# Routing's selections in float16, their keys spread by GpSimd, row constants from the host, the gates' steps placed later

## The chip, the cores and the metric

The kernel runs on one core of a Trainium2 chip. The metric is the device time of one execution in microseconds (us), the median of three runs. The engines are TensorE (PE, matrix products), VectorE (DVE), ScalarE (ACT), GpSimd (POOL) and SyncE (SP, which here only issues transfers). Each runs its own instructions in the order in which they were built, and waits for the others by semaphores.

## The reference, cut to what matters

A Conformer-like block, a block with a product-key mixture of experts (PEER), and two further layers run over 256 tokens of width 1024. The change touches the PEER part alone:

```python
sc = einsum("bshcd,hcnd->bshcn", q, sub_keys)     # 8 heads, 2 halves, 128 keys
s_top, i_top = top_k(sc, 16)
cand = s_top[..., 0, :, None] + s_top[..., 1, None, :]
cand_idx = i_top[..., 0, :, None] * 128 + i_top[..., 1, None, :]
best, pos = top_k(cand.reshape(..., 256), 16)
expert_idx = take_along_axis(cand_idx.reshape(..., 256), pos)
gate = softmax(best)                              # 8 x 16 experts for each token
a = gelu(einsum("ced,cd->ce", u_emb[expert_idx], h))
out = einsum("ce,ced->cd", gate * a, v_emb[expert_idx])
```

## The kernel before

**Stages of the PEER part.** First the *query stage*: 16 chunks of `w_peer_q`, 24 matmuls each. Each weight tile is split into a rounded part `whi` (ACT) and a rest `wlo` (POOL, L145, three buffers); the third matmul of a chunk reads `wlo`. From the chunks PE forms scores `sc` (L922). Then the *U stage*: 128 blocks of 128 experts, 8 matmuls each with tokens 0 to 159 (`ublock`, L1020), each with one 512 KB transfer into a ring of ten buffers. Then the *V stage*: 128 blocks of `vv` in the same way (`vmm`, L1130), added into four PSUM tiles that are first set to zero by a matmul (L1135).

**Tokens 160 to 255** don't go through the blocks. Two `RowGroup`s (64 and 32 tokens) fetch their experts' rows by indirect DMA on POOL (L1627, 512 KB each, 96 of `un` and 96 of `vv`, eight buffers). DVE forms a dot product for each row of `un` (`junk`, L1632) and adds each row of `vv` to `acc` (L1642). `some_rows` steps them along: RU rows for a U block, RV for a V block.

**The routing** is DVE's. For each head and half of the tokens (`tt`) a `unit` finds two top-16 lists (`max`, `max_index`, `match_replace`; values `tv`, indices `iu`), copies the indices as float32 into `tops` (L862), adds the lists to candidates `cd` (L869) and finds their top 16 (`best`, `pos`). For four heads at a time `select` turns `pos` into two digits `f` and looks up the keys: an equality with 0 to 15 (`eq`, L900), a product with `tops` (L904) and a sum over 16 (L906) into `isel` and `jsel`. For `tt` = 0 the product is POOL's. `gates(tt)` forms the expert number `ei` and the gate `ex`.

**What sets the order.** `self.bg` is a list of generators. After each block, `pump` draws from the first of them until the credits of their `yield`s use up a budget: QP for a query chunk, UP[0] for a U block until the rows are asked for, UP[1] after that. `later(n, fn)` puts a step behind the n-th block from then on. By GL these are `ask` and `exp` (GL[0]), `softmax` (GL[1]) and `turn` (GL[2]). `ask` multiplies `ei` by `spread` on PE (L1617), and DVE makes of it the row numbers `idf`, `idx`. `turn` multiplies `ex` by `spread` (L1617) and transposes `jsel`, `isel` and `ex` (L975). From the first U block to the last V block but five, `in_order` pins every engine to the order in which the code was written.

**Behind the routing** DVE and ACT build one-hot factors (`QO`, P, R) for tokens 0 to 159, PE multiplies them (`place`, L1058, 40 groups), and the gates are multiplied into G (L1068, L1035).

Of the kernel before, what the change touches and what calls it, by code (L numbers as in the profile page):

```python
# [15 lines left out]
ALU = mybir.AluOpType  # L16
AX = mybir.AxisListType
# [22 lines left out]
CST = {}  # L40
# [33 lines left out]
QP = 2.8  # L74
UP = (2.1, 1.4)

RU = 0.8
RV = 0.8

GL = (2, 3, 4)  # L80

NT = 4
G_SCALE = 2.0 ** 15


ROWS = ((192, 64), (160, 32))
N = ROWS[-1][0]

# [3 lines left out]
class Kernel:  # L92
# [725 lines left out]
    def peer(self):  # L818
        nc, a = self.nc, self.a
        p2h, p2t, p2q = self.p2h, self.p2t, self.p2q  # L820
# [29 lines left out]
        pos = p2t.tile([128, 2, 8, 16], U32, name="pos")  # L850
        tops = p2t.tile([128, 2, 2, 8, 16], F32, name="tops")

        def unit(tt, h, scs):
# [20 lines left out]

        def select(tt, h0, eng):

            nh = 4
            ps = pos[:, tt, h0:h0 + nh].rearrange("p h s -> p (h s)")
            m = nh * 16
            q = p2t.tile([128, 4, m], U32, name="q", bufs=1)  # L880
            f = p2t.tile([128, 4, m], F32, name="f", bufs=1)
            nc.vector.tensor_scalar(q[:, 0], ps, 4, None, op0=ALU.logical_shift_right)
# [3 lines left out]
            nc.vector.tensor_copy(f, q)  # L886
            z = p2t.tile([128, m], F32, name="z", bufs=1)
            nc.vector.tensor_scalar(z, f[:, 0], 4.0, None, op0=ALU.is_ge)
# [7 lines left out]
            nc.vector.tensor_add(f[:, 1], f[:, 2], f[:, 3])  # L896
            yield 1.2
            for c, dst in ((0, isel), (1, jsel)):
                eq = p2t.tile([128, m, 16], F32, name="eq", bufs=1)
                nc.vector.tensor_tensor(eq, f[:, c, :, None].to_broadcast([128, m, 16]),  # L900
                                  self.iota[:, None, :16].to_broadcast([128, m, 16]), op=ALU.is_equal)
                yield 1.1
                e4 = eq.rearrange("p (h s) a -> p h s a", s=16)
                eng.tensor_tensor(e4, e4, tops[:, tt, c, h0:h0 + nh, None, :].to_broadcast([128, nh, 16, 16]), op=ALU.mult)  # L904
                yield 1.1
                nc.vector.reduce_sum(dst[:, tt, h0:h0 + nh].rearrange("p h s -> p (h s)"), eq, axis=AX.X)  # L906
                yield 1.1

# [179 lines left out]
        pgb = self.open("pgb", side="right")  # L1088
# [488 lines left out]
class RowGroup:  # L1577
# [3 lines left out]
    def __init__(self, k, pool, hn, ei, ex, t0, n):  # L1581
# [9 lines left out]
        self.w = pool.tile([128, n], F32, name=f"w{t0}")  # L1591
        self.fold = pool.tile([128, n], F32, name=f"fold{t0}")
        nc.vector.reduce_sum(self.fold, k.ident.rearrange("p (c t) -> p t c", t=n), axis=AX.X)
        self.own = pool.tile([128, self.copies], F32, name=f"own{t0}")
        nc.vector.reduce_sum(self.own, k.ident.rearrange("p (c t) -> p c t", t=n), axis=AX.X)
# [110 lines left out]
def _constants():  # L1706
# [3 lines left out]
    def put(name, v):  # L1710
        c[:v.shape[0], CST[name]:CST[name] + v.shape[1]] = v
# [134 lines left out]
```

## Time and profile before

| | us |
|---|---|
| median of three runs (lowest to highest) | 1649.78 (1649.56 to 1651.78) |
| the profiled execution's own time | 1649.49 |
| its span | 1647.4 |
| PE busy | 1563.3 |
| DVE busy | 1176.5 |
| ACT, POOL busy | 649.1, 509.9 |

The page gives each engine's busy time, the granted clock of PE and what the transfers moved in slices of the span; queries of the trace give single instructions, waits with their releasers, and stretches. On the span's time scale the query stage ends at about 342 us, the U stage runs from 344 to 674 us and the V stage from 678 to about 980 us. A raw U or V block is recorded twice for each matmul, so "x32" of L1020 is two blocks. Times of a row of a timeline are the start and the duration.

### The profile page before, as it was taken

How to read it: one execution, taken by the hardware profiler on the slowest of the kernel's cores; microseconds unless marked ns; L12 is line 12 of the kernel's file. 1: busy time of each engine (PE TensorE's matmuls, PEld its weight loads, DVE VectorE, ACT ScalarE, POOL GpSimd, SP SyncE). 2: the span in 40 equal slices, each digit the busy share in tenths (PEclk: the TensorE clock that was granted, in tenths of full speed). 3: DMA queues.
4: the chain of work that ended last, by engine and by line, in shares of the span. 5: the costliest groups of instructions: out<-in, count | busy, mean ns of one | idle time of the engine just before them, and what ended most of it. 6: DMA issues, size and time to landing. Idle time of an engine off the chain costs nothing.

```text
span 1647.4 us, 29860 instructions
## 1 busy us (share of the span) xinstructions
PE 1563.3 (95%) x11502; PEld 1485.5 (90%) x11502; DVE 1176.5 (71%) x2549; ACT 649.1 (39%) x1387; POOL 509.9 (31%) x379
## 2 busy tenths in 40 slices
PE   8989979996899999899979999999999999999998
PEld 7878879996899999899979999888999998899986
DVE  6989988999888889644434448866767557676655
ACT  4557645431155444000000015555554455555543
POOL 3734631611576677545354511000000030000000
PEclk9989989998999999999989999999999999999999
DMA  5522336465999999999999965733655576255553
GB/s 184 168 89 91 129 117 214 169 231 222 355 348 400 400 394 388 359 409 409 408 363 408 409 271 182 245 101 98 224 182 186 184 194 210 91 192 182 183 187 114
DMA packets 109389, 398.97 MB, mean 242 GB/s; under 512 B 12484, under 2 KB 12643, under 8 KB 108736
## 3 DMA queue, kind: packets, MB, share of 16 engines
q1 hardware_dynamic: 73872, 266.37, 46.1%
q0 software_dynamic: 35232, 130.64, 21.1%
q8 instruction: 90, 1.47, 0.4%
q14 instruction: 51, 0.42, 0.1%
q10 hardware_dynamic: 144, 0.07, 0.0%
HBM read 394.86 MB, written 6.11 MB: 243 GB/s over the span
## 4 chain that ended last, share of the span: by engine, by line
PE 71%; DVE 17%; DMA 7%; issue 3%; POOL 2%; ACT 1%; SPq 0%; POOLq 0%; DVEq 0%; ACTq 0%
PE ax L1130 12%; PE mm L1020 12%; PE mm L166 11%; PE mm L167 11%; PE mm L168 11%; DMA raw<-vv 3%; DMA wlo<-vv 3%; DVE ax L610 2%; PE mm L234 2%; PE mm L232 1%; PE mm L233 1%; PE ax L463 1%; DVE wlo L147 1%; PE ax L1058 1%; PE ax L1376 1%
## 5 line engine op out<-in xcount | busy, mean ns | idle before, releaser
L143 ACT ACTIVATE whi<-raw 128x1024 fp32r<-128x1024 f32 x275 | 290.2, 1058 | 616.3 <-DMA raw<-wst 302.5
L147 DVE TENSOR_TENSOR wlo<-raw,whi 128x1024 fp32r<-128x1024 f32 x211 | 257.8, 1224 | 106.8 <-ACT whi L143 103.1
L166 PE MATMUL mm<-xgh,whi 128*128 128x256 f32 x1064 | 305.2, 287 | 0.0
L167 PE MATMUL mm<-xgl,whi 128*128 128x256 f32 x1064 | 302.2, 284 | 2.6 <-DVE xgl L406 2.6
L168 PE MATMUL mm<-xgh,wlo 128*128 128x256 f32 x1064 | 302.4, 284 | 0.3 <-DVE wlo L147 0.3
L1642 DVE SCALAR_TENSOR_TENSOR acc<-row,w,acc 128x1024 f32<-128x1024 f32 x94 | 120.8, 1285 | 156.0 <-DMA row<-vv,idx 155.7
L167 PEld LDWEIGHTS mm<-xgl,whi 128*128 128x128 f32 x1064 | 202.8, 191 | 2.9 <-DVE xgl L406 2.8
L166 PEld LDWEIGHTS mm<-xgh,whi 128*128 128x128 f32 x1064 | 202.7, 191 | 1.1 <-issue 0.8
L168 PEld LDWEIGHTS mm<-xgh,wlo 128*128 128x128 f32 x1064 | 202.5, 190 | 0.6 <-DVE wlo L147 0.5
L145 POOL TENSOR_TENSOR wlo<-raw,whi 128x1024 fp32r<-128x1024 f32 x64 | 153.6, 2405 | 137.7 <-ACT whi L143 134.9
L1627 POOL DMA_INDIRECT row<-vv,idx x96 | 120.6, 1256 | 80.0 <-DMA row<-vv,idx 51.8
L1627 POOL DMA_INDIRECT row<-un,idx x96 | 110.0, 1146 | 108.2 <-DVE idf L1621 54.3
L1130 PE MATMUL ax<-G,raw 128*128 128x160 f32 x832 | 125.5, 306 | 6.8 <-DMA raw<-vv 6.8
L1130 PEld LDWEIGHTS ax<-G,raw 128*128 128x128 f32 x832 | 118.6, 195 | 7.6 <-DMA raw<-vv 7.5
L1632 DVE CUSTOM_DVE_ANT_0 junk<-row,h 128x1024 f32<-128x1024 f32 x96 | 120.4, 1254 | 0.5
L1020 PE MATMUL mm<-hn,raw 128*128 128x160 f32 x816 | 118.8, 300 | 0.0
L1020 PEld LDWEIGHTS mm<-hn,raw 128*128 128x128 f32 x816 | 112.8, 190 | 0.0
L167 PE MATMUL mm<-hl,whi 128*128 128x256 f32 x368 | 107.0, 291 | 2.2 <-DVE hl L377 2.1
L1130 PE MATMUL ax<-G,wlo 128*128 128x160 f32 x608 | 93.5, 307 | 11.0 <-DMA wlo<-vv 11.0
L1130 PEld LDWEIGHTS ax<-G,wlo 128*128 128x128 f32 x608 | 88.1, 196 | 12.1 <-DMA wlo<-vv 11.9
L610 DVE SCALAR_TENSOR_TENSOR ax<-u,cw,ax 128x256 f32<-128x256 f32 x227 | 97.7, 481 | 0.7
L166 PE MATMUL mm<-hh,whi 128*128 128x256 f32 x304 | 90.3, 297 | 2.7 <-DVE u L630 2.2
(439 smaller groups left out, 3436.3 us busy)
## 6 DMA issues: line engine op xcount, KB each, us to landing
raw<-wst SPq DMA_DIRECT2D x278, 512.0 KB, 3.6
raw<-ut SPq DMA_DIRECT2D x51, 512.0 KB, 7.3
raw<-vv SPq DMA_DIRECT2D x40, 512.0 KB, 7.3
whi<-ut SPq DMA_DIRECT2D x39, 512.0 KB, 7.0
wlo<-ut SPq DMA_DIRECT2D x38, 512.0 KB, 7.4
whi<-vv SPq DMA_DIRECT2D x32, 512.0 KB, 7.5
wlo<-vv SPq DMA_DIRECT2D x25, 512.0 KB, 7.6
wlo<-vv POOLq DMA_DIRECT2D x13, 512.0 KB, 16.5
```

The source lines that it names most:

```text
L143: nc.scalar.activation(hi, raw, AF.Copy)
L145: nc.gpsimd.tensor_sub(lo, raw, hi)
L147: self.pin = nc.vector.tensor_sub(lo, raw, hi)
L166: nc.tensor.matmul(pt, w[:, s], xs[0][:, k], start=first, stop=False)
L167: nc.tensor.matmul(pt, w[:, s], xs[1][:, k], start=False, stop=False)
L168: nc.tensor.matmul(pt, lo[:, s], xs[0][:, k], start=False, stop=last)
L610: nc.vector.scalar_tensor_tensor(y[:, c] if k == 30 else ps, u[:, c, k:k + T], cw[:, c, k:k + 1], ps, op0=ALU.mult, op1=ALU.add)
L1020: nc.tensor.matmul(pt, raw[:, k * 128:(k + 1) * 128], hn[:, k, :N], start=(k == 0), stop=(k == C - 1))
L1130: nc.tensor.matmul(acc[d // 2][:, d % 2, :N], raw[:, d * 128:(d + 1) * 128], G(i), start=False, stop=False, skip_group_check=True)
L1627: self.k.nc.gpsimd.indirect_dma_start(t, None, table, bass.IndirectOffsetOnAxis(ap=self.idx[:, s:s + 1], axis=0))
L1632: self.k.nc.vector.tensor_tensor_reduce(junk, row, self.h, 1.0, 0.0, ALU.mult, ALU.add, self.a[:, s:s + 1])
L1642: self.k.nc.vector.scalar_tensor_tensor(self.acc, row, w, self.acc, op0=ALU.mult, op1=ALU.add)
```

## The change

The selections are in float16: `f`, `z`, `eq`, and `tops`, which now has each index sixteen times over, so that all operands of the equality and the product lie side by side in memory. POOL writes `tops` (one cast of 128 x 256 for each top-16 list) and a table `num` in place of `iota`. The sum over 16 is four additions. Both halves of the tokens take all of it on DVE. `spread`, `fold` and `own` come from the host in two transfers issued by ACT. `zero` is set by POOL ahead of the stage, and the four matmuls of 512 columns that clear PSUM are sixteen of 128. GL is (5, 6, 7) for (2, 3, 4), UP[1] 1.1 for 1.4, RU 0.85 for 0.8, RV 0.78 for 0.8.

```diff
-UP = (2.1, 1.4)
-RU = 0.8
-RV = 0.8
-GL = (2, 3, 4)
+UP = (2.1, 1.1)
+RU = 0.85
+RV = 0.78
+GL = (5, 6, 7)
...
+        zero = self.cp.tile([128, 128], F32R, name="zero")
+        nc.gpsimd.memset(zero.bitcast(F32), 0.0)
...
-        tops = p2t.tile([128, 2, 2, 8, 16], F32, name="tops")
+        tops = p2t.tile([128, 2, 2, 8, 16, 16], F16, name="tops")
+        num = p2t.tile([128, 16, 16], F16, name="num")
+        nc.gpsimd.tensor_copy(num, self.iota[:, :16, None].to_broadcast([128, 16, 16]))
...
-                nc.vector.tensor_copy(tops[:, tt, c, h], iu)
+                nc.gpsimd.tensor_copy(tops[:, tt, c, h], iu[:, :, None].to_broadcast([128, 16, 16]))
...
-            f = p2t.tile([128, 4, m], F32, name="f", bufs=1)
+            f = p2t.tile([128, 4, m], F16, name="f", bufs=1)
...
-            yield 1.2
+            yield 1.8
             for c, dst in ((0, isel), (1, jsel)):
-                eq = p2t.tile([128, m, 16], F32, name="eq", bufs=1)
-                nc.vector.tensor_tensor(eq, f[:, c, :, None].to_broadcast([128, m, 16]),
-                                  self.iota[:, None, :16].to_broadcast([128, m, 16]), op=ALU.is_equal)
-                yield 1.1
-                e4 = eq.rearrange("p (h s) a -> p h s a", s=16)
-                eng.tensor_tensor(e4, e4, tops[:, tt, c, h0:h0 + nh, None, :].to_broadcast([128, nh, 16, 16]), op=ALU.mult)
-                yield 1.1
-                nc.vector.reduce_sum(dst[:, tt, h0:h0 + nh].rearrange("p h s -> p (h s)"), eq, axis=AX.X)
-                yield 1.1
+                eq = p2t.tile([128, nh, 16, 16], F16, name="eq", bufs=1)
+                nc.vector.tensor_tensor(eq, f[:, c].rearrange("p (h s) -> p h s", s=16)[:, :, None].to_broadcast([128, nh, 16, 16]),
+                                        num[:, None].to_broadcast([128, nh, 16, 16]), op=ALU.is_equal)
+                nc.vector.tensor_mul(eq, eq, tops[:, tt, c, h0:h0 + nh])
+                yield 1.4
+                for n in (8, 4, 2):
+                    nc.vector.tensor_add(eq[:, :, :n], eq[:, :, :n], eq[:, :, n:2 * n])
+                nc.vector.tensor_add(dst[:, tt, h0:h0 + nh], eq[:, :, 0], eq[:, :, 1])
+                yield 0.9
...
-        zeros = pgb.tile([128, 512], F32R, name="zeros")
-        nc.vector.memset(zeros.bitcast(F32), 0.0)
         for q in range(4):
-            nc.tensor.matmul(acc[q].rearrange("p a b -> p (a b)"), zero, zeros, start=True, stop=False, skip_group_check=True)
+            for k in range(4):
+                nc.tensor.matmul(acc[q].rearrange("p a b -> p (a b)")[:, k * 128:(k + 1) * 128], zero, zero, start=True, stop=False, skip_group_check=True)
...
-        self.spread = pool.tile([128, 128], F32, name=f"spread{t0}")
+        c = pool.tile([128, 128 + n + self.copies], F32, name=f"c{t0}")
+        o = CST[f"rows{t0}"]
+        nc.scalar.dma_start(c, k.a["cst"][:, o:o + 128 + n + self.copies])
+        self.spread, self.fold, self.own = c[:, :128], c[:, 128:128 + n], c[:, 128 + n:]
```

Three places of the built programs. On POOL, the end of the query stage, before (the numbers are those of the buffers):

```order
L145 TENSOR_TENSOR wlo_3805<-raw_3802,whi_3804 128x1024
L145 TENSOR_TENSOR wlo_3866<-raw_3863,whi_3865 128x1024
L145 TENSOR_TENSOR wlo_3927<-raw_3924,whi_3926 128x1024
L145 TENSOR_TENSOR wlo_3992<-raw_3989,whi_3991 128x1024
L145 TENSOR_TENSOR wlo_4053<-raw_4050,whi_4052 128x1024
```

and after:

```order
L149 TENSOR_TENSOR wlo_3931<-raw_3928,whi_3930 128x1024
L871 CAST tops_3245<-iu_3794 128x256
L871 CAST tops_3245<-iu_3853 128x256
L149 TENSOR_TENSOR wlo_3996<-raw_3993,whi_3995 128x1024
L871 CAST tops_3245<-iu_3862 128x256
L871 CAST tops_3245<-iu_3921 128x256
L149 TENSOR_TENSOR wlo_4057<-raw_4054,whi_4056 128x1024
L871 CAST tops_3245<-iu_3971 128x256
L871 CAST tops_3245<-iu_3989 128x256
L149 TENSOR_TENSOR wlo_4122<-raw_4119,whi_4121 128x1024
```

The casts stand between the splits of the weight tiles; 15 of them stand ahead of the last split.

On PE, the U stage around the gates of `tt` = 1 (L1617 is `ask` and `turn`, L975 the transposes), before:

```order
L1020 MATMUL mm_4490<-hn_3232,whi_4488 128x160 x8
L1617 MATMUL ax_4499<-ei_4191,spread192_4212 128x128
L1617 MATMUL ax_4505<-ei_4191,spread160_4225 128x128
L1020 MATMUL mm_4525<-hn_3232,wlo_4523 128x160 x8
L1020 MATMUL mm_4552<-hn_3232,raw_4550 128x160 x8
L1617 MATMUL ax_4561<-ex_4192,spread192_4212 128x128
L1617 MATMUL ax_4566<-ex_4192,spread160_4225 128x128
L975 MATMUL ax_4571<-ident_70,jsel_3240 128x128
L975 MATMUL ax_4571<-ident_70,isel_3239 128x128
L975 MATMUL ax_4571<-ident_70,ex_4192 128x128
L1020 MATMUL mm_4594<-hn_3232,whi_4592 128x160 x8
```

and after, where the lines are L1030, L1620 and L985, and `c192` and `c160` hold `spread`:

```order
L1030 MATMUL mm_4576<-hn_3232,raw_4574 128x160 x8
L1620 MATMUL ax_4585<-ei_4195,c192_4212 128x128
L1620 MATMUL ax_4591<-ei_4195,c160_4221 128x128
L1030 MATMUL mm_4610<-hn_3232,whi_4608 128x160 x8
L1030 MATMUL mm_4632<-hn_3232,wlo_4630 128x160 x8
L1620 MATMUL ax_4641<-ex_4196,c192_4212 128x128
L1620 MATMUL ax_4646<-ex_4196,c160_4221 128x128
L985 MATMUL ax_4651<-ident_70,jsel_3242 128x128
L985 MATMUL ax_4651<-ident_70,isel_3241 128x128
L985 MATMUL ax_4651<-ident_70,ex_4196 128x128
L1030 MATMUL mm_4672<-hn_3232,raw_4670 128x160 x8
```

The first group of L1617 stood behind 12 blocks and stands behind 14; the transposes stood behind 14 and stand behind 16. The same transposes of `tt` = 0 stood behind 38 blocks and stand behind 41.

On DVE, from `ei` of `tt` = 1 to the row numbers (`own`, `idf`, `idx`), before:

```order
L953 SCALAR_TENSOR_TENSOR ei_4191<-isel_3239,jsel_3240 128x128
L954 TENSOR_TENSOR ex_4192<-best_3241 128x128
L839 MAX tv_4476<-sc_3712 128x8
L841 MAX_INDEX iu_4477<-tv_4476,sc_3712 128x8
L843 MATCH_REPLACE scw_4475<-tv_4476,sc_3712 128x128
L845 MAX tv_4476<-scw_4475 128x8
L847 MAX_INDEX iu_4477<-tv_4476,scw_4475 128x8
L862 CAST tops_3243<-iu_4477 128x16
L839 MAX tv_4485<-sc_3773 128x8
L1619 TENSOR_TENSOR own_4501<-ax_4499,own192_4210 128x128
L1621 TENSOR_REDUCE idf192_4204<-own_4501 128x64
L1623 CAST idx192_4203<-idf192_4204 128x64
```

and after, the last part of the same way (lines L1622 to L1626 for L1619 to L1623):

```order
L845 MAX tv_4562<-sc_3964 128x8
L847 MAX_INDEX iu_4563<-tv_4562,sc_3964 128x8
L849 MATCH_REPLACE scw_4561<-tv_4562,sc_3964 128x128
L851 MAX tv_4562<-scw_4561 128x8
L853 MAX_INDEX iu_4563<-tv_4562,scw_4561 128x8
L845 MAX tv_4571<-sc_4029 128x8
L1622 TENSOR_TENSOR own_4587<-ax_4585,c192_4212 128x128
L1624 TENSOR_REDUCE idf192_4208<-own_4587 128x64
L1626 CAST idx192_4207<-idf192_4208 128x64
L1622 TENSOR_TENSOR own_4593<-ax_4591,c160_4221 128x128
L1624 TENSOR_REDUCE idf160_4217<-own_4593 128x32
L1626 CAST idx160_4216<-idf160_4217 128x32
```

Between `ei` and `own` stood one top-16 list and the first step of the next. Now five lists and the first step of the sixth stand there, with two full candidate searches, and no cast of `tops`.

## Rows read from the trace of the kernel before

**Rows 1.** The page's parts 1 and 4: busy shares, and the chain of waits by engine.
```profile
PE 1563.3 (95%) x11502; PEld 1485.5 (90%) x11502; DVE 1176.5 (71%) x2549; ACT 649.1 (39%) x1387; POOL 509.9 (31%) x379
...
PE 71%; DVE 17%; DMA 7%; issue 3%; POOL 2%; ACT 1%; SPq 0%; POOLq 0%; DVEq 0%; ACTq 0%
```

**Rows 2.** Windows: stretch, length, busy PE, PEld, DVE, ACT, POOL; clock, DMA, GB/s.
```profile
338.00:374.00 36.00, 35.72 (x274) 35.29 (x272) 34.73 (x198) 13.01 (x29) 0.00 (x0) 1.00 0.78 279
...
430.00:460.00 30.00, 21.15 (x143) 20.54 (x142) 21.39 (x46) 5.94 (x15) 19.67 (x12) 0.83 0.95 344
...
600.00:650.00 50.00, 50.00 (x410) 49.62 (x409) 45.06 (x93) 22.37 (x89) 34.85 (x26) 1.00 1.00 392
...
720.00:770.00 50.00, 50.00 (x370) 50.00 (x369) 21.79 (x17) 0.00 (x0) 25.46 (x24) 1.00 1.03 408
```

**Rows 3.** PE's waits, 338 to 460 and 460 to 690 us: total, times, longest.
```profile
PE ax L1617 <- DVE ei L953: 13.0, 1, 13.0
PE ax L975 <- DVE jsel L906: 4.6, 1, 4.6
PE ax L975 <- DVE ex L967: 4.2, 1, 4.2
...
PE ax L1135 <- DVE zeros L1133: 3.4, 1, 3.4
```

**Rows 4.** Timelines of DVE and POOL in the query stage: start, duration, instruction.
```profile
310.99 2.25 DVE L869 TENSOR_TENSOR cd<-tv 128x48 f32<-128x48 f32 x1
...
347.42 0.15 DVE L862 CAST tops<-iu 128x16 f32<-128x16 uint32 x1
...
310.77 2.41 POOL L145 TENSOR_TENSOR wlo<-raw,whi 128x1024 fp32r<-128x1024 f32 x1 [0.57 <-ACT whi L143]
...
333.69 2.40 POOL L145 TENSOR_TENSOR wlo<-raw,whi 128x1024 fp32r<-128x1024 f32 x1 [0.88 <-ACT whi L143]
```

**Rows 5.** POOL's groups by form: count, busy us, mean ns, idle before.
```profile
L1048 POOL TENSOR_TENSOR R<-QO,gTl 128x512 f16<-128x512 f16 x40 | 66.5, 1662 | 44.3 <-DVE QO L1044 39.4 <-PE mm L1020 2.8 <-DVE G L1035 1.9
L1317 POOL COPY kTb<-kr 32x2048 f32<-32x2048 f32 x1 | 1.9, 1882 | 26.2 <-DVE kr L1316 26.2
```

**Rows 6.** Timeline of DVE: one select, token half 1, and what follows it.
```profile
368.88 0.22 DVE L896 TENSOR_TENSOR f<-f 128x64 f32<-128x64 f32 x1
369.02 1.22 DVE L900 TENSOR_TENSOR eq<-f,iota 128x1024 f32<-128x1024 f32 x1
...
372.78 1.23 DVE L900 TENSOR_TENSOR eq<-f,iota 128x1024 f32<-128x1024 f32 x1
...
386.25 0.29 DVE L953 SCALAR_TENSOR_TENSOR ei<-isel,jsel 128x128 f32<-128x128 f32 x1
...
404.73 0.28 DVE L839 MAX8 best<-cd 128x8 f32<-128x112 f32 x1
...
410.16 0.28 DVE L839 MAX8 best<-cd 128x8 f32<-128x112 f32 x1
```

**Rows 7.** DVE's groups by form, 290 to 700 us, columns as in rows 5.
```profile
L1632 DVE CUSTOM_DVE_ANT_0 junk<-row,h 128x1024 f32<-128x1024 f32 x96 | 120.4, 1254 | 0.5
L1044 DVE TENSOR_TENSOR QO<-io,jiT 128x512 f16<-128x512 f16 x80 | 31.9, 441 | 17.8 <-PE ax L1058 17.4
```

**Rows 8.** PE: timeline (scores, first U block), then line L1617.
```profile
342.24 1.70 PE L922 MATMUL ax<-sk,pq 128*128 128x128 f32 x12
343.78 1.39 PE L1020 MATMUL mm<-hn,raw 128*128 128x160 f32 x9
...
L1617 PE MATMUL ax<-ex,spread x4: 273/276/276, 393.8 to 394.1; 128*128 128x128 f32 x4
```

**Rows 9.** The chain behind the routing, in order of time: start, us, what.
```profile
456.84 7.88 PE mm L1020 x48
465.17 4.40 PE mm L1020 x32
469.57 0.46 PE ax L1058 x8
```

More of the change, by code (lines that the diff above doesn't have):

```diff
@@ L46 @@
 N_CST = _n
+ROWS = ((192, 64), (160, 32))
+for _t0, _w in ROWS:
+    CST[f"rows{_t0}"] = N_CST
+    N_CST += 128 + _w + 128 // _w
 N_WT = 279
@@ L74 @@
 QP = 2.8
-UP = (2.1, 1.4)
-RU = 0.8
-RV = 0.8
-GL = (2, 3, 4)
+UP = (2.1, 1.1)
+RU = 0.85
+RV = 0.78
+GL = (5, 6, 7)
 NT = 4
 G_SCALE = 2.0 ** 15
-ROWS = ((192, 64), (160, 32))
 N = ROWS[-1][0]
@@ L873, in unit, with select @@
             yield from top16(best[:, tt, h], pos[:, tt, h], cd, w)
-        def select(tt, h0, eng):
+        def select(tt, h0):
             nh = 4
@@ L886, in select @@
             nc.vector.tensor_copy(f, q)
-            z = p2t.tile([128, m], F32, name="z", bufs=1)
+            z = p2t.tile([128, m], F16, name="z", bufs=1)
             nc.vector.tensor_scalar(z, f[:, 0], 4.0, None, op0=ALU.is_ge)
@@ L1075, in peer @@
         k = next((k for k, u in enumerate(self.bg) if k and u not in firsts), len(self.bg))
-        self.bg[k:k] = [select(1, 0, nc.vector), select(1, 4, nc.vector), gates(1)]
-        self.bg += [select(0, 0, nc.gpsimd), select(0, 4, nc.gpsimd), gates(0)]
+        self.bg[k:k] = [select(1, 0), select(1, 4), gates(1)]
+        self.bg += [select(0, 0), select(0, 4), gates(0)]
         order = self.in_order()
@@ L1123, in peer @@
         acc = [self.pp.tile([128, 2, T], F32, name="ax", bufs=4) for _ in range(4)]
-        zero = self.cp.tile([128, 128], F32R, name="zero")
-        nc.vector.memset(zero.bitcast(F32), 0.0)
         LAST = 5
@@ L1591, in __init__ @@
         self.w = pool.tile([128, n], F32, name=f"w{t0}")
[L1592 to L1595, printed above, removed]
-        self.spread = pool.tile([128, 128], F32, name=f"spread{t0}")
-        o = t0 % 128
-        nc.vector.tensor_copy(self.spread.rearrange("p (c t) -> p c t", t=n), k.ident[:, None, o:o + n].to_broadcast([128, self.copies, n]))
+        c = pool.tile([128, 128 + n + self.copies], F32, name=f"c{t0}")
+        o = CST[f"rows{t0}"]
+        nc.scalar.dma_start(c, k.a["cst"][:, o:o + 128 + n + self.copies])
+        self.spread, self.fold, self.own = c[:, :128], c[:, 128:128 + n], c[:, 128 + n:]
     def activations(self):
@@ L1745, in _constants @@
     put("onehot", oh)
+    p = np.arange(128)
+    for t0, w in ROWS:
+        put(f"rows{t0}", np.concatenate([p[:, None] == t0 % 128 + p[None] % w, p[:, None] % w == np.arange(w)[None],
+                                         p[:, None] // w == np.arange(128 // w)[None]], 1).astype(f))
     return c
```

## The prediction

> **What bounds the kernel now.** I read the page first. PE is busy for 95% of the span and carries 71% of the chain that ended last, DVE 17% [rows 1], so a change to DVE's routing can only pay where PE stands still or where transfers lag. Second, PE's waits in the PEER part: 13.0 us at L1617 for `ei`, 4.6 and 4.2 us at L975 for `jsel` and `ex`, and 3.4 us for `zeros` at the start of the V stage: 25.2 us in all [rows 3]. Third, the windows. From 338 to 374 us DVE is busy for 34.7 of 36 us, so those waits are DVE's queue of work and not latency; in the window of the waits for `jsel` and `ex` the granted clock is 0.83 and only 344 GB/s are moved; behind the routing PE is busy throughout while 392 GB/s are moved and DVE is busy for 45 of 50 us; in the V stage 408 GB/s are moved, the most of any stretch, and PE waits for loads now and then [rows 2]. So there are three regimes: DVE paces the routing, PE the rest of the U stage (with DVE and transfers close behind), transfers the V stage. Fourth, the timelines: where DVE stands against POOL in the query stage [rows 4], and what one lookup costs [rows 6].
>
> **The lookup.** It now takes 3.76 us (369.02 to 372.78), three passes over 1024 float32. 64 float32 take 0.22 us and 1024 take 1.22 [rows 6], hence 0.155 us fixed and 1.04 ns an element. The float16 equality with the same kind of operands, `QO`, takes 0.441 us for 512 [rows 7]; half the slope gives 0.42, so I take half the slope: 0.69 for 1024, 0.42, 0.29 and 0.22 for the additions of 512, 256 and 128, 0.22 for the last of 64, and 0.03 between any two (the 1.25 between starts less 1.22). That is 2 x 0.69 + 0.42 + 0.29 + 0.22 + 0.22 + 0.18 = 2.71 us: 1.05 less for each of the four lookups ahead of `ei`, 4.2 us. If nothing ran faster it would be 2 x 1.22 + 0.69 + 0.42 + 0.29 + 0.22 + 0.18 = 4.24, a loss of 0.5 us each.
>
> **The casts on POOL.** No row shows one. From below: a POOL copy of 2048 elements takes 1.88 us, so 256 take 0.24; from above: `R`, two inputs of 512, takes 1.66 [rows 5]. I take 0.45 us, near the copy, since a cast has one input. The Trainium skill (GPSIMD Engine Reference, 3.1 Elementwise) gives 1.03 cycles an element for such a body, which at 1.2 GHz is an estimate of 0.22 us plus the dispatch; the sum would stand.
>
> **What is queued behind them.** In the new order 15 casts stand ahead of the last `wlo` of the query stage, and each waits for DVE's list. Before, that `wlo` ran at 333.69 us, while DVE reached its 15th cast at 347.42 [rows 4]. So POOL will wait for DVE, PE's third matmul for `wlo`, and the query stage is paced by DVE. DVE loses 15 casts of about 0.15 us [rows 4], but its two-input additions `cd` wait for POOL: the one at 310.99 took 2.25 us and ended with POOL's split of 310.77 + 2.41 [rows 4], and POOL will be busier. I put the net at 1 us earlier: list 15 at 346.4 (bounds 343 and 351). With the cast, the split of 2.4 and a chunk of 3.3 us (seven splits from 310.77 to 333.69 are 3.27 apart) the stage ends at about 352, 10 us later than the 342.2 of now [rows 8].
>
> **`ei` and the row numbers.** `ei` was formed at 386.25 [rows 6]. Off it: 4.2 for lookups, 1.2 for the six small instructions that built `fold`, `own` and `spread` (at about the 0.22 of a small one [rows 6]), 1 from the query stage, 1 for the other seven casts of 0.15; onto it up to 7 x 0.45 = 3 us and as much again for `cd`s that meet casts: 382 to 385, taken as 384 (bounds 376 and 390). PE starts U blocks at 352 + 1.5 and passes 14 of them, 2.2 us each (two take 4.40 [rows 9]), and 3.8 us of transposes at 388: the wait of 13.0 us is gone. But DVE's order now has four more lists and two candidate searches between `ei` and the row numbers. Four lists and two searches are two units; a unit takes 5.43 us (404.73 to 410.16 [rows 6]), about 5.2 without its casts. Before, 7.5 us lay between `ei` at 386.25 and PE's use of `ex` at 393.8 [rows 6, 8]; with two units more it is 18 us, so PE can use `ex` at 402 (bounds 392 and 410). It arrives behind block 16 at 393 and waits 9 us: the wait is moved, not removed. Before, PE passed here at 393.8 with 14 blocks. Two blocks more are 4.4 us, 8 us later in time: a loss of 4 us so far, and the rows, asked for by the same DVE queue, start some 6 us later.
>
> **The other half.** From `ex` on DVE has left: 1 for the gates, 2.3 units of 5.2, two selects of 12 x 0.22 + 2 x 2.71, 15 dots of 1.25 [rows 7] and 1 us: 49 us, to 451. PE runs 25 blocks, 55 us, to 457, so it does not wait: the waits of 4.6 and 4.2 us go, with the slow restart behind them (three blocks in 7.88 us instead of 6.6 [rows 9]). What is late next is PE itself. Before, PE went on at 456.8 with 38 blocks; now at 457 with 41: 6.6 us, and 1.3 for the restart: **nearly 8 us ahead**.
>
> **To the end of the V stage.** 87 blocks and 40 placements of 0.46 us [rows 9] are 210 us, to 667; 90 blocks from 456.8, with the slow restart, are 218, to 674. Without the wait for `zeros` the V stage starts at 668 instead of 677.7. But 1.85 instead of 1.8 transfers of 0.524 MB for a block, at 2.2 + 0.46 x 40/87 = 2.41 us a block, ask for 402 GB/s, against 392 carried now and 408 at most [rows 2], and DVE's 45 of 50 us become about 47, as the same work has less time. I take off 1 us for that. In the V stage only what transfers allow is kept. Four rows fewer are left for it (97 issued ahead of its first POOL load instead of 93), 4 x 1.28 = 5 us (0.524 MB at 408 GB/s), but its ring is filled less far. Of the 9.7 us I keep 8, and 2 for the rows: **10 us**. The two transfers on ACT, 128 x 776 bytes at most, hide behind the first U block, and the sixteen clearing matmuls have the columns of the four. Sum: 1649.5 - 10 = 1639.5, and with the median 0.3 us above the profiled execution's 1649.49, 1640 us.
>
> **The rivals.**
>
> *POOL's casts hold up DVE: slower.* Place: the query stage and the units behind it. 28 casts stand ahead of the first `ex`, and each that meets a `cd` delays DVE by its own length, while each `cd` that starts first delays POOL. Every 0.1 us above my 0.45 costs up to 2.8 us there, so from about 0.8 us a cast eats the 10 us. At 1.15, between the bounds, it is 20 us: 1659. For it: the 2.25 us of a `cd` of 48 elements, which alone would take no more than the 0.22 of 64 [rows 4, 6]. Against it: the copy's rate [rows 5]. The Trainium skill (SBUF - State Buffer, Who interferes with whom) calls the port pair of DVE and GpSimd an exclusive lock, held for the whole instruction, which a DVE instruction with two SBUF inputs needs when GpSimd reads SBUF. The row of 310.99 agrees, and by that rule this rival's mechanism is certain, and only its price open.
>
> *The waits meet less often than I think.* POOL waits for DVE, so DVE runs alone in those times, and lists come faster. Then `ex` is ready at 393, the lower bound, PE does not wait behind block 16, and the U stage gains 8 us more, of which transfers let through about half at 402 GB/s wanted: 1634, or 1629 if the ring of ten buffers carries it. For it: the 2.25 us that a `cd` now loses go when POOL stands idle [rows 4]; against it: POOL is idle there only as long as DVE is late, and outside the query stage DVE's 34.7 of 36 us are work [rows 2].
>
> *Float16 does not run at twice the rate.* 1.53 us more a lookup, 6.1 us ahead of each `ex`: PE passes block 41 at 463, and 4 us of gain are left: 1646. Against it: `QO` [rows 7].
>
> **How the numbers follow.** The forecast, 1632 to 1647, has a chance of 0.64; the costly casts 0.14; the luckier meeting 0.14; float16 without its rate 0.08. Two runs of this kernel can be told apart from about 0.2%, 3.3 us. Faster by that: nearly all of the forecast, the third case, half of the fourth, less some for the place in the V stage where the gain may be lost again: 0.75. Within it: 0.12. Slower: the first rival, 0.13. The range takes the forecast's bounds, half of the luckier case and part of the costly one: 1629 to 1653.
>
> **What would show it.** Right: splits of `wlo` on POOL that wait for casts, and a query stage that ends 7 to 12 us later; no wait for `ei`; one of 4 to 12 us for `ex` behind block 16; none at the transposes of `tt` = 0; equalities of 0.65 to 0.75 us; PE at the first V block near 668 us; over 400 GB/s from 460 us on. Wrong: casts of 0.8 us or more, `cd`s of over 2 us by the dozen, PE waiting for U loads behind the routing, or a V stage longer by what the U stage gained.

## The result, and the profile after

The changed kernel takes **1633.49 us** (median; 1632.27 to 1633.68) against 1650.78 us for the kernel before beside it: a ratio of 0.9885, with a 95% interval from 0.9856 to 0.9914. The forecast was 1640 us. The profiled execution took 1632.27 us, its span is 1629.3 us, 18.1 less than before. By the records most of the gain is made by the end of the V stage: the sums behind it (L1176 before, L1183 now) start at 968.8 us instead of 984.6, 15.8 of the 18.1 us. The other 2.3 lie behind the V stage, where nothing was changed: 662.8 us before and 660.5 now, and 660.0 to 663.4 in the profiles of all kernels shown here.

Busy shares and the chain by engine, which answer to [rows 1]: DVE lost 11 us of work, and its share of the chain fell from 17 to 15%, while that of DMA rose from 7 to 12%.

```profile
PE 1560.1 (96%) x11514; PEld 1481.1 (91%) x11514; DVE 1165.5 (72%) x2535; ACT 646.5 (40%) x1383; POOL 519.1 (32%) x409
...
PE 68%; DVE 15%; DMA 12%; issue 3%; POOL 1%; ACT 1%; SPq 0%; POOLq 0%; DVEq 0%; ACTq 0%
```

The four windows of [rows 2], in the same columns:

```profile
338.00:374.00 36.00, 33.59 (x252) 32.87 (x251) 34.18 (x170) 13.26 (x31) 10.37 (x14) 0.95 0.66 225
430.00:460.00 30.00, 30.00 (x224) 30.00 (x223) 17.23 (x41) 8.04 (x22) 10.89 (x11) 1.00 1.03 409
600.00:650.00 50.00, 50.00 (x413) 49.62 (x412) 48.49 (x96) 22.66 (x91) 38.45 (x28) 1.00 1.03 407
720.00:770.00 50.00, 49.71 (x363) 49.12 (x362) 21.84 (x17) 0.00 (x0) 26.03 (x23) 1.00 1.03 409
```

From 430 to 460 us, where PE stood still for 9 of 30 us at a granted clock of 0.83, it is now busy throughout at 1.00, and 409 GB/s are moved instead of 344. From 600 to 650 us the transfers carry 407 GB/s instead of 392, with DVE at 48.5 of 50 us. From 338 to 374 us POOL now has work: the query stage reaches into that window.

PE's waits from 338 to 460 us, then from 460 to 690 us, which answer to [rows 3]:

```profile
PE ax L1620 <- DVE ex L977: 4.8, 1, 4.8
PE mm L172 <- POOL wlo L149: 2.4, 2, 2.0
...
PE ax L1138 <- DMA wlo<-vv: 5.7, 1, 5.7
```

The waits of 13.0, 4.6, 4.2 and 3.4 us are gone. In their place are 4.8 us for `ex`, 2.4 for the last splits of the query stage, and 5.7 for the load of the first V block. But the first U block now starts at 354.0 instead of 343.8 us. The start of the U stage and the routing's waits of PE together came to 343.8 + 21.8 = 365.6 us and now come to 354.0 + 4.8 = 358.8: of 17.0 us of waits 10.2 went into a later start, and 6.8 are won.

The lookup and the cast from 290 to 460 us, by form (count, busy us, mean ns, idle before), beside [rows 5, 6]:

```profile
L910 DVE TENSOR_TENSOR eq<-f,num 128x1024 f16<-128x1024 f16 x8 | 5.5, 686 | 0.1
L912 DVE TENSOR_TENSOR eq<-eq,tops 128x1024 f16<-128x1024 f16 x8 | 5.5, 692 | 0.6
...
L915 DVE TENSOR_TENSOR eq<-eq 128x512 f16<-128x512 f16 x8 | 3.4, 422 | 0.1
...
L871 POOL CAST tops<-iu 128x256 f16<-128x256 uint32 x32 | 13.0, 406 | 63.5 <-DVE iu L853 61.9 <-PE mm L171 1.6
```

Start of the V stage on PE (start, duration): the clearing matmuls stand where [rows 3] had the wait for `zeros`; the first V block waits for its load.

```profile
665.54 2.20 PE L1142 MATMUL ax<-zero 128*128 128x128 f32 x16
...
673.46 3.92 PE L1138 MATMUL ax<-G,wlo 128*128 128x160 f32 x16 [5.72 <-DMA wlo<-vv]
```

### The profile page after: what moved, and what is told of

It reads as the page before. It is cut to its first block, busy times and chain, and to the rows that moved or that the text cites. A ratio compares the mean times of both kernels' runs of the same rounds, so it can differ in the third digit from the quotient of the medians.

```text
span 1629.3 us, 29917 instructions
## 1 busy us (share of the span) xinstructions
PE 1560.1 (96%) x11514; PEld 1481.1 (91%) x11514; DVE 1165.5 (72%) x2535; ACT 646.5 (40%) x1383; POOL 519.1 (32%) x409
## 4 chain that ended last, share of the span: by engine, by line
PE 68%; DVE 15%; DMA 12%; issue 3%; POOL 1%; ACT 1%; SPq 0%; POOLq 0%; DVEq 0%; ACTq 0%
PE mm L1030 15%; PE mm L170 11%; PE mm L171 11%; PE mm L172 11%; PE ax L1138 6%; DMA wlo<-vv 3%; DMA raw<-vv 3%; DMA row<-vv,idx 3%; DMA whi<-vv 2%; DVE ax L614 2%; PE ax L467 1%; PE mm L238 1%; PE mm L236 1%; PE mm L237 1%; DVE wlo L151 1%
## 5 line engine op out<-in xcount | busy, mean ns | idle before, releaser
L1630 POOL DMA_INDIRECT row<-vv,idx x96 | 127.9, 1332 | 102.8 <-DMA row<-vv,idx 68.6
L1030 PE MATMUL mm<-hn,raw 128*128 128x160 f32 x816 | 120.9, 303 | 0.0
L1030 PEld LDWEIGHTS mm<-hn,raw 128*128 128x128 f32 x816 | 114.8, 193 | 0.0
L1138 PE MATMUL ax<-G,whi 128*128 128x160 f32 x608 | 91.4, 300 | 2.7 <-DMA whi<-vv 2.6
```

The lines of the kernel that those rows point to most:

```text
L1030: nc.tensor.matmul(pt, raw[:, k * 128:(k + 1) * 128], hn[:, k, :N], start=(k == 0), stop=(k == C - 1))
L1138: nc.tensor.matmul(acc[d // 2][:, d % 2, :N], raw[:, d * 128:(d + 1) * 128], G(i), start=False, stop=False, skip_group_check=True)
L1630: self.k.nc.gpsimd.indirect_dma_start(t, None, table, bass.IndirectOffsetOnAxis(ap=self.idx[:, s:s + 1], axis=0))
```

## The experiments

Two of the changed kernels were run in two sets each, on different chips, and their medians repeat within 0.6 us (1633.49 and 1634.09; 1627.22 and 1626.95), while that of the kernel before was 1650.8, 1653.1, 1651.3 and 1656.0. So medians are compared here, and ratios to the kernel before beside each are given with their 95% intervals. Single executions of one kernel lie up to 8.5 us apart, so a difference of 2 us between two medians is not settled. Edits are shown shortened, without the lines that only prepare them.

**1. Gates' steps back at 2 to 4 blocks.**

```
-GL = (5, 6, 7)
+GL = (2, 3, 4)
```

> The changed kernel with the gates' steps back at 2, 3 and 4 blocks. Theory A (lookup and casts alone now bring `ei` in time): `ei` at 381.5 us, PE there behind 11 blocks at 381 to 382, a wait under 2 us; `ex` at about 389, a wait of 2 to 4 us; row numbers and the first row some 8 us earlier than with 5 to 7; no wait above 5 us at the second transposes: 1628 to 1633 us. Theory B (the moved steps carry the gain): waits of 10 us or more in sum come back at `ei`, `ex` and the second transposes: 1638 to 1643 us.

Measured: **1627.22 us**, and 1626.95 in a second set, where it was the base of two others (ratios 0.9841, 0.9821 to 0.9861, and 0.9829, 0.9813 to 0.9846).

> The changed kernel with the gates' steps at 2, 3 and 4 blocks once more, as the base of the two behind it: 1627 us within 2, 1.4 to 1.6% less than the kernel before.

PE's wait, the first row on POOL, and the window behind it:

```profile
PE ax L1620 <- DVE ex L977: 1.6, 1, 1.6
...
389.22 1.03 POOL L1630 DMA_INDIRECT row<-un,idx  x1 [0.42 <-PE mm L1030]
...
400.00:430.00 30.00, 30.00 (x223) 30.00 (x222) 28.40 (x104) 4.26 (x14) 16.91 (x17) 1.00 1.02 405
```

The same window of the changed kernel:

```profile
400.00:430.00 30.00, 30.00 (x210) 30.00 (x209) 27.61 (x106) 4.49 (x16) 13.51 (x16) 0.94 0.93 354
```

Theory A holds, with a time just below its 1628 to 1633 us and a smaller wait for `ex` than its 2 to 4 us; start and waits come to 355.8 + 1.6 = 357.4 us. `ei` is there at 383.3 us, PE comes at 383.7 behind 11 blocks and does not wait; `ex` costs 1.6 us instead of 4.8; the first gather goes out at 389.22 instead of 397.52 us. The second half's transposes (449.9 us, 40 blocks) do not wait either. So with the shorter lookup the moved steps *cost* 6 to 7 us: they put off the row numbers. The two kernels' executions don't overlap (1625.5 to 1630.2 against 1632.2 to 1635.9).

**2. The moved steps and rates without the shorter lookup.** On the kernel before, lookups in float32 and `zeros` kept:

```
-GL = (2, 3, 4); UP = (2.1, 1.4); RU = 0.8; RV = 0.8
+GL = (5, 6, 7); UP = (2.1, 1.1); RU = 0.85; RV = 0.78
```

> The kernel before with the numbers of the change alone: gates' steps 5 to 7 blocks behind, UP 1.1, RU 0.85, RV 0.78; lookups in float32, `zeros` kept. Theory (blocks fill the wait): PE arrives for `ei` behind 14 blocks, the wait of 13.0 us falls to about 7; `ex` comes at about 404 us; the waits at the second transposes go. PE passes the second transposes at about 459 us with 41 blocks instead of 456.8 with 38, 5 us ahead, and the V stage keeps its losses: 1643 to 1646 us. Rival (the gain is that of the shorter lookup): 1649 to 1652 us.

Measured: 1638.53 us (ratio 0.9908, 0.9887 to 0.9928), 4.5 us below the theory's range. PE's waits in the routing:

```profile
PE ax L1617 <- DVE ex L967: 8.5, 1, 8.5
PE ax L1617 <- DVE ei L953: 6.5, 1, 6.5
```

They are 15.0 us instead of the 21.8 of [rows 3]; `ei` is waited for as the theory had it, and PE passes `ex` at 403.5 us. What the theory lacked comes behind: from 460 to 660 us 407 GB/s are moved, not 390. Start and waits come to 344.8 + 15.0 = 359.8 us: this kernel wins 5.8 us there, about as much as the whole change (6.8) and less than the lookup with the old steps (8.2). The steps and the lookup fill the same wait, and don't add. In time, these numbers alone bring 0.92% of the change's 1.15%; all the rest of it, the lookup, the constants from the host and the clearing of PSUM, brings 5 us on top of them (1638.5 to 1633.5). What the lookup brings with every number as before was not run: the kernel of experiment 1 has the new rates and no `zeros`. The constants from the host and UP[1] were not tested by themselves either.

**3. The rates of rows as before.**

```
-RU = 0.85
-RV = 0.78
+RU = 0.8
+RV = 0.8
```

> The changed kernel with RU and RV at 0.8, as before: rows are asked for 0.05 slower for each U block. Theory (ledger of transfers: from about 430 us on the ring carries 408 GB/s whatever stands in it, so the end is set by the bytes moved before the V stage): 112 blocks x 0.05 = 5.6 rows of 0.524 MB are left for the V stage, 2.9 MB or 7 us at 408 GB/s: some 393 GB/s from 460 to 660 us, the same PE up to 666 us, the V stage 5 to 7 us longer, 1638 to 1641 us. Rival (the gain is PE's U stage alone, and the row rate is hidden): 1633 us within 1.5.

Measured: 1639.31 us (ratio 0.9927, 0.9902 to 0.9951); the changed kernel beside it 1634.09.

> The changed kernel itself, beside the next three on one chip, as their base: 1633 us within 2, and 1.1% less than the kernel before.

The window from 460 to 660 us, of the kernel before, of this one, and of the changed one:

```profile
460.00:660.00 200.00, 200.00 (x1635) 198.56 (x1634) 172.53 (x356) 99.75 (x370) 142.52 (x107) 1.00 1.00 390
```

```profile
460.00:660.00 200.00, 200.00 (x1639) 198.52 (x1638) 174.85 (x361) 98.56 (x372) 146.00 (x108) 1.00 1.01 394
```

```profile
460.00:660.00 200.00, 200.00 (x1639) 198.52 (x1639) 182.12 (x370) 97.02 (x372) 152.71 (x113) 1.00 1.02 407
```

PE is busy for all of the 200 us in each: what the ring carries here is what it is asked for. The U stage ends at 666.2 us as with 0.85, and the V stage takes 309.2 us instead of 303.3 (305.0 in the second profile of the changed kernel). So some 5 us of the gain are the row rate, at the size that the theory gave (with 393 GB/s forecast for the window). The executions of this kernel scatter from 1634.9 to 1642.3 us, and the intervals of the two ratios (the changed kernel's is 0.9875 to 0.9908) overlap a little; the rates in the windows and the length of the V stage carry the reading.

**4. The place of `zeros`.** In the V stage of the kernel before stands a wait that the prediction did not read. POOL, PE and the window from 800 to 900 us:

```profile
829.73 0.56 POOL L1147 DMA_DIRECT2D xo<-park  x1 [19.12 <-PE ax L1130]
...
839.09 3.30 PE L1130 MATMUL ax<-G,wlo 128*128 128x160 f32 x11 [9.99 <-DMA wlo<-vv]
...
800.00:900.00 100.00, 89.85 (x636) 89.21 (x635) 40.45 (x32) 0.00 (x0) 44.62 (x43) 0.93 0.99 390
```

After:

```profile
800.00:900.00 100.00, 95.70 (x697) 94.50 (x696) 40.58 (x33) 0.00 (x0) 48.65 (x43) 1.00 1.03 409
```

POOL waited 19.1 us to issue the load of `xo`, until PE had ended the 64th V block, and the loads behind it on the same queue came late: PE stood still for 10.0 us, and only 390 GB/s were moved. In the built program of before, `G1` lay at bytes 86304 to 127264 of a partition, with `zeros` above it, and the pool of `xo` reached up to 87392: 1088 bytes in common (of two other tiles of that pool), so `xo`, the pool's first tile, waited for `G1`'s last reader. Without the 2 KB of `zeros` `G1` begins at 88352, and the wait is gone. One kernel puts 2 KB back into the changed kernel, another takes `zeros` out of the one before (with `zero` set early by GpSimd and the sixteen clearing matmuls, as in the change):

```
+        pad = pgb.tile([128, 512], F32, name="pad")
+        nc.gpsimd.memset(pad[:, :1], 0.0)
```

```
-        zeros = pgb.tile([128, 512], F32R, name="zeros")
-        nc.vector.memset(zeros.bitcast(F32), 0.0)
```

> The changed kernel with a tile of 2 KB a partition back in the pool `pgb`, where `zeros` stood; nobody reads it. Theory (placement): without `zeros`, G1 lies 2 KB higher and no longer overlaps the pool of `xo`, so POOL's load of `xo` need not wait for the last reader of G1; with the pad it waits again, for the first 64 V blocks. Expected: a wait of 10 to 20 us on POOL before `xo`, PE starved for 6 to 10 us right behind the 64th V block, a stretch of 20 us with some 310 instead of 408 GB/s, and 4 to 6 us more: 1637 to 1640 us. Nothing changes up to 665 us. Rival (the V stage gained by its rates of rows alone): no wait, and 1633.5 us within 1.5.

> The kernel before with one edit of the change: no `zeros` tile, `zero` set early by GpSimd, sixteen clearing matmuls of 128 columns. Theory (placement and wait): the 3.4 us at the start of the V stage go, and the 19.1 us of POOL before `xo` with the 10.0 us of PE behind them, worth about 5 us of transfers: 1641 to 1643 us. Rival (the V stage is bound by transfers, so a start 3.4 us earlier and a POOL wait in it are worth nothing): 1648 to 1650 us.

With the pad: 1635.71 us (ratio 0.9889, 0.9866 to 0.9911). The wait, PE's stop and the loss of transfers are back:

```profile
820.58 0.56 POOL L1156 DMA_DIRECT2D xo<-park  x1 [22.45 <-PE ax L1140]
...
830.54 4.63 PE L1140 MATMUL ax<-G,wlo 128*128 128x160 f32 x16 [10.60 <-DMA wlo<-vv]
...
800.00:900.00 100.00, 89.40 (x639) 89.16 (x639) 39.29 (x31) 0.00 (x0) 40.28 (x42) 0.93 0.98 384
```

The mechanism is as the theory says, but its price is not shown: 2 us more than the changed kernel by the medians, and the intervals of the ratios lie over each other, though the profiled V stage ends at 974.3 us instead of 968.8. `zeros` taken from the kernel before gave 1646.58 us (ratio 0.9954, 0.9941 to 0.9968), between its theory and its rival: 4 to 9 us less than the medians of the kernel before, 6.5 less than the one beside it. Its profile can't show that gain, as the execution profiled was the slowest of the seven (1650.48 us): 409 GB/s are moved from 800 to 900 us, but the V stage ends no earlier (986.0 us), since less had been moved before it (below). So the edit pays, by some 2 to 7 us; a closer figure these runs don't give.

**5. The casts on VectorE.**

```
-nc.gpsimd.tensor_copy(tops[:, tt, c, h], ...)
+nc.vector.tensor_copy(tops[:, tt, c, h], ...)
```

> The changed kernel with the 32 casts on VectorE instead of GpSimd. Theory (POOL waits for DVE's lists in the query stage): no split waits for a cast, the first U block comes at 344 to 346 us instead of 354; each cast costs DVE about 0.3 us (the cast of 256 elements in the select takes 0.29), 9 us in 32, but the 16 additions of 48 elements, which now take 1.05 us in the mean beside POOL, fall to about 0.4 and give 10 us back: `ei` within 3 us of 381.5, a wait for `ei` of 4 to 8 us on PE, and 1630 to 1637 us in all. Rival (GpSimd's casts are what makes the lookup pay): `ei` 5 us later or more, 1638 to 1645 us. Rival (the lock is costly): `ei` 5 us earlier or more, under 1630 us.

Measured: 1640.85 us (ratio 0.9935, 0.9918 to 0.9952). PE's waits, the cast and the additions:

```profile
PE ax L1620 <- DVE ex L977: 10.5, 1, 10.5
PE ax L1620 <- DVE ei L963: 8.6, 1, 8.6
...
L871 DVE CAST tops<-iu 128x256 f16<-128x256 uint32 x32 | 14.6, 457 | 0.6
...
L878 DVE TENSOR_TENSOR cd<-tv 128x48 f32<-128x48 f32 x16 | 10.7, 666 | 0.0
L878 DVE TENSOR_TENSOR cd<-tv 128x64 f32<-128x64 f32 x16 | 3.4, 212 | 0.0
```

The cast takes DVE 0.457 us and not 0.3, 14.6 us in all; `ei` comes at 388.8 us instead of 381.5, the first row at 404.4. The first U block starts at 346.5 instead of 354 us, and PE stands still for 19.1 us later on: together 365.6 us, as before the change. The rival holds that GpSimd's casts make the lookup pay: with the casts on VectorE the kernel is no faster than that of experiment 2 (1638.5 us), which has the same steps and rates and the float32 lookup.

**6. Each cast twice on GpSimd.**

```
+for _ in range(2):
     nc.gpsimd.tensor_copy(tops[:, tt, c, h], ...)
```

> The changed kernel with every cast on GpSimd done twice: 32 x 0.41 = 13 us more work there, the result unchanged. It measures the slope of the prediction's first rival. Theory (only the additions of 48 elements that meet a cast wait): 12 of the 16 stand ahead of the first use of `ex`, each up to 0.4 us longer: `ex` 3 to 5 us later, the first row too, PE's wait for `ex` 8 to 10 us, and 1636 to 1640 us. Rival (the prediction's slope, 2.8 us for each 0.1 us of a cast): 1645 us. Rival (GpSimd's idle 62 us swallow it): 1634 us within 1.5.

Measured: 1632.2 us (ratio 0.9858, 0.9841 to 0.9874): nothing lost. The additions and the casts of this kernel, then the additions of the changed one:

```profile
L879 DVE TENSOR_TENSOR cd<-tv 128x48 f32<-128x48 f32 x16 | 12.1, 759 | 0.0
L879 DVE TENSOR_TENSOR cd<-tv 128x64 f32<-128x64 f32 x16 | 7.9, 494 | 0.0
...
L872 POOL CAST tops<-iu 128x256 f16<-128x256 uint32 x64 | 26.0, 406 | 51.4 <-DVE iu L853 49.3 <-issue 0.2
```

```profile
L878 DVE TENSOR_TENSOR cd<-tv 128x48 f32<-128x48 f32 x16 | 16.8, 1053 | 0.0
L878 DVE TENSOR_TENSOR cd<-tv 128x64 f32<-128x64 f32 x16 | 3.3, 203 | 0.0
```

The last rival holds, with a time 0.3 us below its band: GpSimd's idle time swallows 13 us. What DVE pays is the same in both, 20 us in 32 additions (12.1 + 7.9 and 16.8 + 3.3), against 13.1 before (0.41 us each in the mean): so it isn't the length of the cast that holds up `cd`. POOL and DVE in the query stage of the changed kernel show what does:

```profile
336.51 0.40 POOL L871 CAST tops<-iu 128x256 f16<-128x256 uint32 x1 [1.12 <-DVE iu L853]
336.88 2.39 POOL L149 TENSOR_TENSOR wlo<-raw,whi 128x1024 fp32r<-128x1024 f32 x1
342.01 0.40 POOL L871 CAST tops<-iu 128x256 f16<-128x256 uint32 x1 [1.56 <-PE mm L171]
342.37 2.35 POOL L149 TENSOR_TENSOR wlo<-raw,whi 128x1024 fp32r<-128x1024 f32 x1
...
337.50 1.83 DVE L878 TENSOR_TENSOR cd<-tv 128x48 f32<-128x48 f32 x1
339.92 0.20 DVE L878 TENSOR_TENSOR cd<-tv 128x64 f32<-128x64 f32 x1
343.02 1.76 DVE L878 TENSOR_TENSOR cd<-tv 128x48 f32<-128x48 f32 x1
```

The cast waits for DVE's list (the trace puts the second one shown down to PE, which came last), POOL's split of `wlo` follows it at once, and DVE's next two-input addition starts 0.3 to 0.7 us into that split and ends with it: 336.88 + 2.39 = 339.27 us against 337.50 + 1.83 = 339.33. All eight units whose additions lie between 307 and 349 us look like that, 1.76 to 2.13 us each; before, four did, 1.60 to 2.25 us. With the casts taken off GpSimd (experiment 5) it is four again, 1.49 to 2.35 us, and 14.1 us in all. So the cast sets the meeting, and the split its price. The Trainium skill (SBUF - State Buffer, Who interferes with whom) has the lock that the prediction cited; the trace agrees with it, in each of these pairs.

**7. More rows sooner.** On the kernel of experiment 1 (steps at 2 to 4): six more rows as soon as the numbers are there; then GpSimd's share of the V loads moved by three; then both, with 5 to 7 blocks for the second half of the tokens.

```
-                some_rows(RU)
+                some_rows(RU + burst)
+                burst = 0
```
```
-nc.gpsimd if nv % 4 == 0 else nc.sync
+nc.gpsimd if nv % 4 == 3 else nc.sync
```

> The changed kernel with the gates' steps at 2, 3 and 4 blocks and, new, six rows more asked for as soon as the row numbers are there: seven gathers in a row from about 389 us, into the eight buffers that are there. Ledger theory: between 385 and 400 us some 230 to 250 GB/s are moved with steps 2 to 4; six rows of 0.524 MB more by about 405 us are 3.1 MB, of which transfers after 400 us, at 405 GB/s already, give some back: 4 to 6 us less than the 1627 us of steps 2 to 4, 1621 to 1624 us. Rival (DVE's dots, six of them 1.25 us earlier, hold up the second half's lists, or U blocks wait for loads): 1627 us or more.

> Steps at 2, 3 and 4 blocks, and GpSimd's queue issues the V blocks whose number leaves 3 instead of 0 when divided by 4: the very first V block then comes by SyncE's queue and isn't behind gathers that wait for DVE. Theory (that place is PE's wait of 8.6 us for the first V load): the wait falls under 2 us. Ledger theory: transfers ran at 402 to 409 GB/s there already, so the wait is only moved: 1626 us, at most 2 us gained. Rival (PE's start of the V stage sets the end): 1619 to 1622 us.

> Seven gathers in a row once the numbers are there, first V block by SyncE's queue, the gates' steps at 2, 3 and 4 blocks for the first half of the tokens and 5, 6 and 7 for the second. Theory (in burst_6 PE's waits of 6.3 us for the second half's `jsel` and `ex` ate what the earlier rows gave): they go, the U stage ends at 662 us instead of 667, transfers stand 1.5 MB ahead of steps 2 to 4 without the burst: 1621 to 1625 us. Rival (DVE has no room for dots that early, and something else of it comes late): 1627 us or more.

Measured: 1633.05 us (0.9893, 0.9876 to 0.9909), 1626.82 us (0.9836, 0.9809 to 0.9864) and 1631.23 us (0.9844, 0.9828 to 0.9861): against 1627 us a loss, a draw, and a loss of 4 us whose interval overlaps that of the base (0.9813 to 0.9846). In both kernels with the burst the rival holds; for the moved V loads the ledger's 1626 us does. With the burst PE waits for DVE in the second half again, since the dots that came forward stand ahead of the lists (`ei` of the second half at 449.3 us instead of 443.9):

```profile
PE ax L985 <- DVE ex L977: 3.2, 1, 3.2
PE ax L1621 <- DVE ex L977: 1.6, 1, 1.6
PE ax L985 <- DVE jsel L916: 1.5, 1, 1.5
```

Of these, 4.7 us are the second half's (the 1.6 at L1621 is the first half's); the split lags left 1.8 of them, but the U stage still ended 3 to 5 us later than without the burst (664.7 against 661.9 and 659.6 us). With GpSimd's V loads moved, the first block no longer waits; the fourth does, which is now the first that POOL issues, behind gathers that wait for DVE. POOL's issue of that load, and PE's wait for it:

```profile
664.12 0.59 POOL L1018 DMA_DIRECT2D whi<-vv  x1
...
674.62 4.64 PE L1138 MATMUL ax<-G,whi 128*128 128x160 f32 x16 [7.97 <-DMA whi<-vv]
```

**The ledger of transfers.** From the first U block to the end of the V stage every kernel moves the same: 367 GB/s x 640.8 us = 235.2 MB before, 382 x 614.8 = 234.9 after, and 234.4 to 235.6 in the others. So what was moved by 700 us tells how much is left for a stage that moves 409 GB/s at most (in these profiles). Each row is worked out from the profiles, as the mean rate of a window times its length; a profile is one execution, so the median beside it can be another (for `zeros` alone by 4 us):

| kernel | first row, us | moved by 700 us, MB | V stage starts / ends, us | median, us |
|---|---|---|---|---|
| `zeros` alone | 391.6 | 123.2 | 678.2 / 986.0 | 1646.6 |
| before | 390.3 | 125.0 | 677.7 / 984.6 | 1650.8 to 1656.0 |
| rows as before | 398.8 | 126.9 | 666.2 / 975.4 | 1639.3 |
| casts on VectorE | 404.4 | 127.3 | 674.0 / 979.8 | 1640.9 |
| steps and rates only | 401.1 | 129.0 | 671.8 / 975.4 | 1638.5 |
| changed, two profiles | 397.5, 399.7 | 130.4, 129.6 | 665.5, 667.0 / 968.8, 972.0 | 1633.5, 1634.1 |
| pad of 2 KB | 397.6 | 130.4 | 665.1 / 974.3 | 1635.7 |
| casts twice | 396.1 | 130.8 | 663.0 / 968.2 | 1632.2 |
| steps 2 to 4, two profiles | 389.2, 386.9 | 132.8, 133.7 | 661.9, 659.6 / 964.1, 962.2 | 1627.2, 1627.0 |
| burst | 387.1 | 134.0 | 666.6 / 967.0 | 1633.1 |
| V loads moved | 385.1 | 134.4 | 657.9 / 964.6 | 1626.8 |
| burst and split lags | 386.2 | 135.0 | 664.7 / 966.2 | 1631.2 |

A megabyte is 2.44 us at 409 GB/s. From the mean of the changed kernel (130.0 MB, 970.4 us) the rule gives 977 to 978 us for 127 MB (measured 975.4 and 979.8), 962 for the steps at 2 to 4 (964.1 and 962.2), and for the three kernels with the hole at `xo` (before, steps and rates only, pad) the same with 5 us on top: before 982.5 + 5 against 984.6. All lines up to 133.7 MB fall within 3 us of it. Before to after, 5.4 MB are 13 us, and the hole (401 instead of 409 GB/s from 700 to 950 us, 2 MB) 5 more: 18, where 15.8 were measured. From 134 MB on the rule breaks: the last three end 5 to 8 us later than it says. There transfers run out first: from 930 to 950 us these three move 229 to 241 GB/s, and the changed kernel 406. So PE, which starts its V blocks no earlier or waits at their start, is what ends last.

## Why the prediction came out as it did

The sign, the place and most of the mechanism were right; the gain was forecast at 10 us and came to 17. What the forecast did not ask is which part of the change carries the gain: the moved steps, which it never priced by themselves, cost 6 to 7 us once the lookup is shorter (experiment 1), though with the rates they bring most of the gain without it (experiment 2). Point by point:

1. **The lookup**, forecast 2.71 us: right. It takes 2.75 (from 368.40 to 371.15 us), with equalities of 0.686 us and additions of 0.422, 0.292 and 0.225. The third rival, float16 without its rate, falls.
2. **The casts**, forecast 0.45 us between 0.24 and 1.66: 0.406. Right in size. The estimate of 0.22 us plus the dispatch, from the Trainium skill (GPSIMD Engine Reference, 3.1 Elementwise), would leave 0.19 for the latter; no run here takes the two apart.
3. **What is queued behind them.** Forecast: splits that wait for casts, list 15 at 346.4, the first U block at 353.5 us. Measured: 61.9 us of POOL's idle time behind DVE's lists, 34.7 of them from 380 us on, list 15's cast at 347.09, the first U block at 354.0. Right, as far as the end: the net of 1 us that DVE was to gain by list 15 came to 0.3 (347.09 against 347.42), as its additions lost 7 us more to POOL's splits over the whole routing (experiment 6).
4. **`ei` and `ex`.** Forecast 384 (376 to 390) and 402 (392 to 410): 381.5 and 397.6. PE came at 388.0 without a wait, as forecast, and waited 4.8 us for `ex` behind block 16, where 9 were forecast with bounds of 4 to 12. The first row left at 397.5, 7 us later, where 6 were forecast. The wait was moved, as the prediction said; it didn't see that with this lookup it need not have been (experiment 1).
5. **The other half.** DVE forecast ready at 451 us: the second `ei` was there at 437.4. Of these 13.6 us, 4.4 are the earlier `ex`, and some 6 are five of the 15 dots, which come behind `ei` and not ahead of it; the last 3 are not traced further. DVE then did these dots and stood idle for 7.3 us until the exponentials came by their count of blocks. PE passed the second transposes at 455.7 with 41 blocks, without a wait; forecast 457.
6. **To the end of the V stage: the step that was mis-sized.** V stage at 665.5 instead of 668, 12.2 us ahead and not 9.7; the 1 us taken off for transfers wasn't needed, since they carry the 402 GB/s asked for, and more (407 from 460 to 660 us). And the V stage, which was to give back 1.7 us of the lead and gain 2 by rows, got 3.6 us shorter. The row rate is worth some 5 us (experiment 3), not 2: the sum had the 5 and cut it for a ring filled less far. PE does wait 5.7 us for the first V block, yet from 654 to 700 us 387 GB/s are moved, against 357 before and 372 with the old row rate. Where rows start earlier, with the steps at 2 to 4, it is 403 GB/s, and moving the wait was a draw there (experiment 7). The hole in front of `xo`, 2 to 7 us, was not seen at all: the window of 720 to 770 us stood for the whole stage, and 50 us later, from 820 to 840 us, 313 GB/s were moved.

**The rivals.** The first, costly casts, falls by its price: of its slope of 2.8 us for 0.1 us of a cast nothing shows (experiment 6); its mechanism, DVE held by POOL, is there, with the splits as the price. The second, luckier meetings, had the time (1634 us) by luck and half of the reason: the ring carries 402 GB/s, but `ex` was not at 393, and the additions met a split in eight places and not in four.

## What to carry to other kernels

When two stages share one saturated resource, count its bytes from the first moment at which it could be busy: here what was asked for early counted fully, as long as the transfers ended last, and the wait for the first V block, a symptom only, gave nothing when it was moved. Look at the whole stage in equal slices before taking one window for it, and ask of a tile that is removed what its place in memory held up. A step that is moved to hide a wait has to be tried again at its old place once the wait itself has become shorter: here the same change with its steps left where they were is 6 to 7 us faster, as the waits for `ei` and `ex` that the steps were to hide are then 1.6 us.

## What had not been expected of the hardware

A cast of 0.41 us on GpSimd that waits for VectorE brings the two engines into step: the split of 2.4 us behind it then met VectorE's next two-input addition in each of eight pairs (1.76 to 2.13 us instead of 0.20), where 4 of the 32 additions met a split before, and 4 with the casts on VectorE. The same cast of 256 unsigned integers to float16 takes 0.406 us on GpSimd and 0.457 on VectorE. And with gathers of rows and whole blocks mixed, on two queues, the transfers of the kernel of experiment 1 moved 408 GB/s in the mean from 400 to 860 us, although PE stood still for 8.6 us of it at the first V block.
